# A two-layer hybrid encoder on one core: the phases as a list of smaller steps in another order

## The chip, the cores and the metric

The kernel runs on one core of a Trainium2 chip. The metric is the time of one execution on the device in microseconds, as a median of several runs. A core has five engines that work side by side: TensorE (PE, matrix multiply; its weight loads have a row of their own, PEld), VectorE (DVE), ScalarE (ACT), GpSimd (POOL) and SyncE (SP), whose queue issues nearly all DMA transfers here. Each engine takes its instructions in the order in which the program has them.

## What is computed

Two groups of requests, "prompt" (p, 1024 tokens) and "sample" (s, 512 tokens), go through the same two layers of width 1024. They share the weights and nothing else.

```python
for l in range(DEPTH):                       # 2 layers
    h = rms_norm(x, norm_g[l])
    u = h @ w_in[l]                          # one projection to all branches
    mk, mv = split(rms_norm(mem, ...) @ w_mem_kv[l])
    if l % 2 == 0:
        y1 = short_conv(gb, gc, hc, conv_w)  # gated convolution
        y2 = window_attention(q, k, v, sink) # "swa", 2 kv heads
    else:
        y1 = dense_gqa(q, k, v)              # "ax", 2 kv heads
        y2 = diff_attention(dq, dk, dv, ...) # "diff", 4 heads, two softmaxes each
    ym = memory_attention(mq, mk, mv)        # "mem", 256 memory tokens
    x = x + (concat(y1, y2, ym) * silu(z)) @ w_out[l]
```

## The kernel before

Every fp32 product is made of three matmuls on a high and a low part (whi, wlo of the weights; hi, lo of the activations). A tile that comes by DMA as alo or wraw is split: ScalarE casts it to the high part (line 186), VectorE or GpSimd subtracts (line 187).

The work is written as calls at the end of trunk_kernel. in_proj(g, l, hs, ids, ahead, hfs) makes chunks of 256 columns of the input projection for group g and layer l: kv, q0, q1, z0 to z8, mq, in layer 0 also gch and gbz (the convolution), in layer 1 dk, dq and dv (each 0 and 1). hfs chooses halves of 512 tokens. Each chunk loads four wraw tiles (load_w). q, k, dq, dk and mq go through prep (norm and rotary tables on ScalarE, VectorE and GpSimd), are transposed on TensorE (stT, store_stack), split, and stored to DRAM (st_...); v and dv are stored by put_v, z by silu2.

The attention steps swa, ax, diff and mem_attn load k, v and q from there (k, v, qhh, qll), make scores (s), their maxima (nm, VectorE), exponentials (e, ScalarE), transposes (pT), splits (pthi, ptlo) and outputs (o), and store y. diff(g, hd, half) does head hd, or one half of its query tokens. They are marked urgent. out_proj loads y (load_y, into alo and ahi), multiplies by w_out and adds x. norm_steps makes the normalized and transposed activations for the next layer in twelve small steps per 512 tokens (four loads and scalings, eight groups of four transposes hT, one PSUM buffer, with hg or ht behind); they wait in a list BG. The projections call between() at a quarter of each group of matmuls, which takes one store_stack from TAIL or one step from BG.

ahead is a function that in_proj, out_proj or mem_kv calls ahead of its last chunk: it empties BG and TAIL and loads the next activations. The activation ring "act" has 16 tiles, k and v rings three each, wraw three, the PSUM ring "x" one.

The calls are the program's order as written; a scheduler then makes each engine's order, and takes an urgent step first when it is ready, so that projections fill the room that attention leaves on TensorE.

Of the kernel before, what the change touches and what calls it, by code (L numbers as in the profile page):

```python
# [68 lines left out]
def trunk_kernel(ctx: ExitStack, tc: tile.TileContext, a: dict, dbg=None):  # L69
# [883 lines left out]
    in_proj("p", 0, hp, range(0, 3))  # L953
    swa("p", 0)
    in_proj("p", 0, hp, range(3, 5))
    swa("p", 1)
    in_proj("p", 0, hp, range(5, 7))
    mem_attn("p", 0)
    in_proj("p", 0, hp, range(7, 15), ahead("y0", lambda: load_y("p", 0, 0, slice(0, 4))))
    out_proj("p", 0, 0, nxt["y0"] + load_y("p", 0, 0, slice(4, 5)), ahead("y1", lambda: load_y("p", 0, 1)))  # L960
    BG.extend(norm_steps(rows_of(S["p", "x1"]), put_dram(S["p", 1, "h"], 0, g1)))
    bg(3)
    out_proj("p", 0, 1, nxt["y1"], ahead("m", lambda: load_act(S["m", 1, "h"], range(4))))
    BG.extend(norm_steps(rows_of(S["p", "x1"], 1), put_dram(S["p", 1, "h"], 512, g1)))
    bg(3)
    mem_kv(1, nxt["m"], ahead("hp", lambda: load_h("p", 1)))
    hp = nxt["hp"]
    in_proj("p", 1, hp, range(0, 3))
    ax("p", 0)
    in_proj("p", 1, hp, range(3, 5))  # L970
    ax("p", 1)
# [17 lines left out]
    diff("p", 3, 0)  # L989
    mem_attn("p", 1, 0)  # L990
    out_proj("s", 0, 0, nxt["ys"] + [ym0])
    flush()
    bg(len(BG))
    hs = [new_h()]
    BG.extend(norm_steps(rows_of(S["s", "x1"]), put_act(hs[0], g1)))
    bg(3)
    RATE[0] = 1
# [1 line left out]
    RATE[0] = 1
    diff("p", 2, 1)  # L1000
    diff("p", 3, 1)
    mem_attn("p", 1, 1)
# [9 lines left out]
    diff("s", 3)  # L1012
    ym = [ring(sb, [128, 2, 512], F32R, "xh", f"ym{i}") for i in range(2)]
    mem_attn("s", 1, ys=ym)
    out_proj("p", 1, 0, load_y("p", 1, 0), ahead("y1", lambda: load_y("p", 1, 1)))
    out_proj("p", 1, 1, nxt["y1"], ahead("ys", lambda: load_y("s", 1, 0, slice(0, 4))))
    out_proj("s", 1, 0, nxt["ys"] + [ym])
# [111 lines left out]
```

## Time and profile before

| | us |
|---|---|
| median of 3 runs | 2139.87 (2139.24 to 2140.7) |
| the profiled execution | 2138.74 |
| its span in the trace | 2136.9 |
| TensorE busy in the span | 2055.3 (96%) |
| VectorE busy | 1548.2 (72%) |
| ScalarE busy | 1113.2 (52%) |
| GpSimd busy | 976.6 (46%) |

A busy time is the union of an engine's instructions. The table by stretch gives the same for stretches of the span, with the number of instructions, the granted TensorE clock as a share of full speed, the share of the DMA engines and their rate. The table of waits names the instruction that waited, its line, what ended the wait and its line, the total, the number and the longest. A timeline has the start, the time taken, the engine, the line and the instruction, and in brackets the idle time ahead of it with what ended that.

### The profile page before, as it was taken

To read this page: it belongs to the slowest core of one execution; us is meant where nothing else is said; L and a number is where in the kernel's file an instruction comes from. 1 tells how busy PE (TensorE), PEld (TensorE's weight loads), DVE (VectorE), ACT (ScalarE), POOL (GpSimd) and SP (SyncE) were. 2 spreads that over 40 slices of the span, in tenths; PEclk is the share of its full clock that TensorE was granted. 3 is DMA by queue.
4 is the path that set the end of the run, shared out by engine and by line. 5 is a ranking of instruction groups with operands and counts; after the bars stand their busy time and mean duration, and the time that the engine had idled before them with its cause. 6 is when DMAs were issued, how large, how long until landed. Compare 5 with 4: busy or idle time off the path is not lost. (4 is left out here: it accounts for less than half of the span.)

```text
span 2136.9 us, 40415 instructions
## 1 busy us (share of the span) xinstructions
PE 2055.3 (96%) x14056; PEld 1887.4 (88%) x14056; DVE 1548.2 (72%) x3340; ACT 1113.2 (52%) x2634; POOL 976.6 (46%) x994
## 2 busy tenths in 40 slices
PE   6999999999999999999999999998998999989999
PEld 6999888889999899999998888886997898979999
DVE  8779867654545688976989988777879876866532
ACT  5545433443343466665666655456566565644521
POOL 6753512342124564743745553333345775643311
...
GB/s 232 203 246 198 215 104 89 121 105 221 253 235 211 167 94 100 124 105 131 114 104 204 179 202 161 118 163 226 170 208 172 195 176 191 137 207 242 200 180 105
DMA packets 321052, 363.69 MB, mean 170 GB/s; under 512 B 27984, under 2 KB 227408, under 8 KB 320848
## 3 DMA queue, kind: packets, MB, share of 16 engines
...
q8 instruction: 111, 1.82, 0.4%
...
## 5 line engine op out<-in xcount | busy, mean ns | idle before, releaser
L187 POOL TENSOR_TENSOR wlo<-wraw,whi 128x512 fp32r<-128x512 f32 x182 | 249.1, 1371 | 359.7 <-ACT whi L186 350.4
L682 ACT ACTIVATE e<-s,nm 128x512 f32<-128x512 f32 (+1 forms) x416 | 264.6, 639 | 224.2 <-DVE nm L680 163.5
L186 ACT CAST whi<-wraw 128x512 fp32r<-128x512 f32 x388 | 237.2, 622 | 274.7 <-PE po L311 91.4
L591 DVE TENSOR_TENSOR ptlo<-pT,pthi 128x512 fp32r<-128x512 f32 x352 | 237.6, 682 | 48.8 <-ACT pthi L590 47.5
L680 DVE TENSOR_REDUCE nm<-s 128x1 f32<-128x512 f32 (+1 forms) x368 | 247.7, 681 | 26.5 <-PE s L584 25.3
L309 PE MATMUL po<-whi,ahi 128*128 128x256 f32 x896 | 255.1, 285 | 4.8 <-ACT ahi L186 2.5
L310 PE MATMUL po<-wlo,ahi 128*128 128x256 f32 x896 | 254.3, 285 | 0.0
L311 PE MATMUL po<-whi,alo 128*128 128x256 f32 x896 | 253.5, 285 | 0.6 <-DVE alo L187 0.5
L590 ACT CAST pthi<-pT 128x512 fp32r<-128x512 f32 x352 | 199.8, 587 | 98.1 <-PE pT L670 55.0
L187 DVE TENSOR_TENSOR wlo<-wraw,whi 128x512 fp32r<-128x512 f32 x206 | 165.7, 805 | 105.6 <-ACT whi L186 104.4
L309 PE MATMUL pa<-whi,ahi 128*128 128x256 f32 x768 | 219.7, 286 | 1.8 <-ACT ahi L186 1.1
L310 PE MATMUL pa<-wlo,ahi 128*128 128x256 f32 x768 | 219.3, 286 | 0.3 <-POOL wlo L187 0.3
L311 PE MATMUL pa<-whi,alo 128*128 128x256 f32 x768 | 219.1, 285 | 0.2 <-DVE alo L187 0.2
L223 POOL TENSOR_TENSOR rs<-ss,mhalf 128x8 f32<-128x8 f32 (+2 forms) x108 | 139.7, 1293 | 163.9 <-DVE ss L219 97.2
L583 PE MATMUL s<-k,qhh 128*128 128x512 f32 (+2 forms) x512 | 192.4, 381 | 12.4 <-ACT e L682 10.0
L584 PE MATMUL s<-k,qll 128*128 128x512 f32 (+2 forms) x512 | 183.3, 364 | 4.4 <-DMA qll<-st_s1dq 1.3
L309 PEld LDWEIGHTS po<-whi,ahi 128*128 128x128 f32 x896 | 171.4, 191 | 7.0 <-ACT ahi L186 3.7
L311 PEld LDWEIGHTS po<-whi,alo 128*128 128x128 f32 x896 | 171.1, 192 | 2.2 <-DVE alo L187 1.2
L310 PEld LDWEIGHTS po<-wlo,ahi 128*128 128x128 f32 x896 | 171.4, 192 | 1.0
L323 PE MATMUL pb<-h,whi 128*128 128x512 f32 x432 | 171.2, 396 | 0.0
L325 PE MATMUL pb<-h,wlo 128*128 128x512 f32 x432 | 170.4, 395 | 0.0
L324 PE MATMUL pb<-h,whi 128*128 128x512 f32 x432 | 170.3, 394 | 0.0
...
## 6 DMA issues: line engine op xcount, KB each, us to landing
...
alo<-y_p SPq DMA_DIRECT2D x20, 512.0 KB, 4.8
...
k<-st_p1dk SPq DMA_DIRECT2D x14, 512.0 KB, 4.8
v<-dv_p SPq DMA_DIRECT2D x14, 512.0 KB, 5.7
...
```

Source lines behind the costliest of these rows:

```text
L186: nc.scalar.copy(out=out_hi, in_=src)
L187: lo_eng.tensor_tensor(out=out_lo, in0=src, in1=f32(out_hi), op=ALU.subtract)
L309: nc.tensor.matmul(out=out, lhsT=h, rhs=wh, start=(k == 0), stop=False)
L310: nc.tensor.matmul(out=out, lhsT=h, rhs=wl, start=False, stop=False)
L311: nc.tensor.matmul(out=out, lhsT=l_, rhs=wh, start=False, stop=(k == n - 1))
L323: nc.tensor.matmul(out=out, lhsT=wh, rhs=h, start=(k == 0), stop=False)
L583: nc.tensor.matmul(out=out, lhsT=q2[0], rhs=k, start=True, stop=False)
L584: nc.tensor.matmul(out=out, lhsT=q2[1], rhs=k, start=False, stop=True)
L590: nc.scalar.copy(out=hi, in_=ps)
L591: nc.vector.tensor_tensor(out=lo, in0=ps, in1=f32(hi), op=ALU.subtract)
L680: nc.vector.tensor_reduce(out=nm, in_=s, axis=AXL.X, op=ALU.max, negate=True)
L682: nc.scalar.activation(out=e[:, j, :], in_=s[:, j, :], func=ACTF.Exp, bias=nm[:, j:j + 1], accum_out=su[:, j:j + 1],)
```

## The change

The calls become a list of strings, STEPS, that a function step reads in turn. What was a whole call is cut smaller and put in another order; the functions that do the work are the same.

- diff p 0 runs as two halves, the second first, with its own loads of k and v for each half.
- In the prompt group's layer 1, dv0 comes ahead of ax p 1, dq0 and z4 behind it, dq1 and dv1 behind the halves of diff, dk1 behind z6 of half 0.
- In the sample group's layer 0, diff p 1 1 moves from between q1 and swa s 1 to behind mem s 0; the load of the prompt group's second half (load p 1 1) ahead of gbz3.
- In the sample group's layer 1, dv0 comes first, ahead of mem p 1 1; dk0 stands beside q1 and z2; dk1, dq1, mq0, dv1, z8 and z6 follow diff s 1 in this order.
- The loads that ahead made ahead of the last chunk are steps of their own (load, loady), mostly a chunk earlier. What ahead did ahead of z8 of the prompt group's half 1 (empty BG) is gone, so that the norm's steps for the sample group spread over mq0, z8 and dv0.

```diff
+STEPS = [
+    "in p 0 kv0+q0+z4", "swa p 0", "in p 0 q1+z6+mq0", "swa p 1", "in p 0 z8", "mem p 0",
+    "in p 0 gch0+gbz0+gch1+gbz1+gch2+gbz2", "loady p 0 0 0 4", "in p 0 gch3+gbz3", "loady p 0 0 4 5",
+    "loady p 0 1", "out p 0 0", "norm p 0", "out p 0 1", "norm p 1", "load m", "load p 1 01", "memkv m",
+    "in p 1 kv0+q0+z0", "ax p 0", "in p 1 q1+z2+dk0+dv0", "ax p 1", "in p 1 dq0+z4", "diff p 0 1", "diff p 0 0",
+    "diff p 1 0", "in p 1 dq1+dv1", "in p 1 z6 0", "in p 1 dk1", "in p 1 mq0+z8 0", "load s 0 0",
+    "in s 0 kv0+q0+z4", "swa s 0", "in s 0 q1+z6", "swa s 1", "in s 0 mq0+z8", "mem s 0", "diff p 1 1",
+    "in s 0 gch0+gbz0+gch1+gbz1+gch2+gbz2+gch3", "load p 1 1", "in s 0 gbz3", "loady s 0 0 0 4", "in p 1 z6 1",
+    "diff p 2 0", "diff p 3 0", "mem p 1 0", "out s 0 0", "norm s", "in p 1 mq0+z8 1", "diff p 2 1", "diff p 3 1",
+    "in s 1 dv0", "mem p 1 1", "in s 1 kv0+q0+z0", "ax s 0", "in s 1 q1+dk0+z2+dq0", "ax s 1", "in s 1 z4",
+    "diff s 0", "diff s 1", "loady p 1 0", "in s 1 dk1+dq1+mq0+dv1+z8+z6", "diff s 2", "diff s 3", "mem s 1",
+    "loady p 1 1", "out p 1 0", "loady s 1 0 0 4", "out p 1 1", "out s 1 0",
+]
...
-    in_proj("p", 1, hp, range(5, 9))
-    diff("p", 0)
-    diff("p", 1, 0)
-    in_proj("p", 1, hp, range(9, 12))
-    in_proj("p", 1, hp, range(12, 15), ahead("hs", lambda: load_h("s", 0)), hfs=[0])
-    hs = nxt["hs"]
-    in_proj("s", 0, hs, range(0, 3))
-    swa("s", 0)
-    in_proj("s", 0, hs, range(3, 5))
-    diff("p", 1, 1)
-    swa("s", 1)
-    in_proj("s", 0, hs, range(5, 7))
...
-    mem_attn("s", 0, ys=ym0)
-    in_proj("s", 0, hs, range(7, 15), ahead("h1", lambda: load_half("p", 1, 1)))
-    in_proj("p", 1, [None, nxt["h1"]], range(12, 13), ahead("ys", lambda: load_y("s", 0, 0, slice(0, 4))), hfs=[1])
-    diff("p", 2, 0)
...
-    in_proj("p", 1, [None, nxt["h1"]], range(13, 15), ahead("", lambda: None), hfs=[1])
...
-    in_proj("s", 1, hs, range(0, 3))
-    ax("s", 0)
-    in_proj("s", 1, hs, range(3, 5))
-    ax("s", 1)
-    in_proj("s", 1, hs, range(5, 9))
-    diff("s", 0)
-    diff("s", 1)
-    in_proj("s", 1, hs, range(9, 15))
-    diff("s", 2)
...
+    def settle():
+
+        bg(len(BG))
+        flush()
...
+        elif op == "loady":
+            settle()
+            l, hf = int(x[0]), int(x[1])
+            part = slice(int(x[2]), int(x[3])) if len(x) > 2 else slice(0, 5)
+            YS.setdefault((g, l, hf), []).extend(load_y(g, l, hf, part))
```

What that does to the engines' orders is seen at three places. Each row is one instruction, or some equal ones that follow each other: its line, what it does, out<-in and the size.

The first is SP's queue around out s 0 0, where alo<-y_s are the loads of the attention outputs of the sample group's layer 0 (y_s_119), st_p1dq and dv_p belong to diff p 2 0, and y_s_119<-yo stores the last outputs. Before:

```order
L106 DMA y_s_119<-yo 128x2x128
L106 DMA zg_p_106<-z_19135 128x512
L106 DMA wraw<-in_w_out_dram 128x512 x2
L106 DMA alo<-y_s_119 128x1024
L106 DMA wraw<-in_w_out_dram 128x512
L106 DMA qhh<-st_p1dq_96 64x2x256
L106 DMA k<-st_p1dk_98 128x1024
L106 DMA qhh<-st_p1dq_96 64x2x256
L106 DMA qll<-st_p1dq_96 64x2x256 x2
L106 DMA alo<-y_s_119 128x1024
```

After:

```order
L119 DMA wraw<-in_w_out_dram 128x512 x2
L119 DMA alo<-y_s_119 128x1024
L119 DMA qhh<-st_p1dq_96 64x2x256 x2
L119 DMA qll<-st_p1dq_96 64x2x256 x2
L119 DMA alo<-y_s_119 128x1024
L119 DMA wraw<-in_w_out_dram 128x512 x3
L119 DMA alo<-y_s_119 128x1024
L119 DMA y_s_119<-yc 128x512
L119 DMA wraw<-in_w_out_dram 128x512
L119 DMA alo<-y_s_119 128x1024
```

The attention's stores (yo) stood between the loads before; now the last of them are further up, and the loads stand close to each other, with only the convolution's store (yc) ahead of the last.

The second is TensorE's order where the norm of the sample group's second layer (hT) meets the second half of diff p 2 (s, pT) and mem p 1 (o). Before:

```order
L253 MATMUL hT<-ident_r,x 128x128 x4
L583 MATMUL s<-k,qhh 128x512
L584 MATMUL s<-k,qll 128x512
L887 MATMUL o<-pthi,v 128x512
L887 MATMUL o<-ptlo,v 128x512
L887 MATMUL o<-pthi,v 128x512
L799 MATMUL pT<-ident_r,e 128x128 x7
L887 MATMUL o<-ptlo,v 128x512
L583 MATMUL s<-k,qhh 128x512
L584 MATMUL s<-k,qll 128x512
L253 MATMUL hT<-ident_r,x 128x128 x4
```

After (h_20858 and its like are tiles of the activations that this norm makes, pa is in s 1 dv0):

```order
L266 MATMUL hT<-ident_r,x 128x128 x4
L322 MATMUL pa<-whi,h_20858 128x256
L323 MATMUL pa<-wlo,h_20858 128x256
L900 MATMUL o<-pthi,v 128x512
L900 MATMUL o<-ptlo,v 128x512
L900 MATMUL o<-pthi,v 128x512
L900 MATMUL o<-ptlo,v 128x512
L898 MATMUL pT<-ident_r,e 128x128 x4
L812 MATMUL pT<-ident_r,e 128x128
L324 MATMUL pa<-whi,h_20859 128x256
L322 MATMUL pa<-whi,h_20858 128x256
L323 MATMUL pa<-wlo,h_20858 128x256
```

The groups of transposes stand further apart, and matmuls of dv0 that read what they make now stand between them.

The third is SP's queue where the sample group's dq1 is stored (st_s1dq_123<-sthi, stlo) and the weights of the chunks behind it are loaded (wraw<-in_w_in). Before:

```order
L106 DMA st_s1dq_123<-sthi 128x1x256 x2
L106 DMA st_s1dq_123<-stlo 128x1x256 x2
L106 DMA zg_s_133<-z_25191 128x512
L106 DMA qhh<-st_s1dq_123 64x2x256 x2
L106 DMA qll<-st_s1dq_123 64x2x256 x2
L106 DMA st_s1dq_123<-sthi 128x1x256 x2
L106 DMA st_s1dq_123<-stlo 128x1x256 x2
L106 DMA qhh<-st_s1dq_123 64x2x256
L106 DMA y_s_134<-yo 128x256
L106 DMA qhh<-st_s1dq_123 64x2x256
L106 DMA qll<-st_s1dq_123 64x2x256 x2
L106 DMA zg_s_133<-z_25246 128x512
```

After (st_s1dq_122 is dq0, stored long ahead):

```order
L119 DMA wraw<-in_w_in_dram 128x512 x3
L119 DMA y_s_134<-yo 128x2x128
L119 DMA wraw<-in_w_in_dram 128x512
L119 DMA st_s1dq_123<-sthi 128x1x256 x2
L119 DMA st_s1dq_123<-stlo 128x1x256 x2
L119 DMA qhh<-st_s1dq_122 64x2x256 x2
L119 DMA qll<-st_s1dq_122 64x2x256 x2
L119 DMA zg<-zg_s_133 128x2x128
L119 DMA y_s_134<-yo 128x2x128
L119 DMA wraw<-in_w_in_dram 128x512
```

The loads of dq1 stood right behind its stores before, with the weights behind them; now the loads behind the stores are those of another tensor, and weights stand on both sides.

## Rows read from the trace of the kernel before

**Rows 1.** The page: span, and each engine's busy time, share and instructions.

```profile
span 2136.9 us, 40415 instructions
...
PE 2055.3 (96%) x14056; PEld 1887.4 (88%) x14056; DVE 1548.2 (72%) x3340; ACT 1113.2 (52%) x2634; POOL 976.6 (46%) x994
```

**Rows 2.** By stretch: length, busy PE, PEld, DVE, ACT, POOL, clock, DMA share, GB/s.

```profile
0.00:660.00 660.00, 629.98 (x4073) 572.71 (x4074) 444.12 (x921) 292.44 (x674) 253.61 (x253) 0.99 0.61 186
660.00:1130.00 470.00, 466.75 (x3408) 440.04 (x3407) 370.47 (x858) 282.96 (x668) 260.69 (x284) 1.00 0.45 128
1130.00:1230.00 100.00, 96.24 (x643) 86.72 (x642) 91.58 (x208) 66.17 (x162) 54.85 (x49) 1.00 0.60 179
1230.00:1440.00 210.00, 204.05 (x1137) 173.43 (x1136) 172.35 (x411) 107.42 (x270) 87.62 (x80) 1.00 0.57 162
1450.00:1490.00 40.00, 31.71 (x180) 24.66 (x179) 30.87 (x76) 24.49 (x61) 10.52 (x14) 1.00 0.73 218
1597.00:1627.00 30.00, 22.03 (x96) 15.59 (x94) 29.84 (x53) 20.89 (x50) 16.76 (x14) 0.84 0.71 209
1660.00:1710.00 50.00, 47.19 (x333) 43.32 (x332) 40.20 (x84) 29.03 (x79) 39.88 (x43) 1.00 0.68 188
1803.00:1815.00 12.00, 9.45 (x69) 8.74 (x68) 4.90 (x12) 4.52 (x11) 3.48 (x5) 1.00 0.92 263
1880.00:1905.00 25.00, 19.12 (x128) 17.83 (x127) 10.10 (x22) 8.44 (x19) 4.13 (x6) 0.93 0.74 213
...
1130.00:2040.00 910.00, 865.61 (x5805) 781.88 (x5804) 707.49 (x1528) 518.63 (x1262) 448.06 (x446) 0.99 0.63 184
```

**Rows 3.** Waits of TensorE, 1440 to 1500: waiter, releaser, total, times, longest.

```profile
PE po L309 <- ACT ahi L186: 2.5, 2, 1.4
PE o L887 <- DVE yo L891: 2.4, 1, 2.4
```

**Rows 4.** Timeline of TensorE in the last out_proj: start, time taken, instruction.

```profile
2091.86 0.28 PE L309 MATMUL po<-whi,ahi 128*128 128x256 f32 x1
2091.98 0.28 PE L310 MATMUL po<-wlo,ahi 128*128 128x256 f32 x1
```

**Rows 5.** Waits of TensorE, 1590 to 1700.

```profile
PE hT L253 <- DVE hg L264: 3.5, 2, 3.1
```

**Rows 6.** Timeline of VectorE beside the norm, from 1611.

```profile
1611.45 0.68 DVE L264 TENSOR_TENSOR hg<-hT,gains 128x512 f32<-128x512 f32 x1
...
1616.31 0.41 DVE L279 TENSOR_TENSOR h<-hg,h 128x256 fp32r<-128x256 f32 x1
```

**Rows 7.** Timeline of SP's queue, 1886 to 1896.

```profile
1886.83 1.25 SPq L106 DMA_DIRECT2D st_s1dq<-sthi  x2
...
1894.13 1.45 SPq L106 DMA_DIRECT2D wraw<-in_w_in_dram  x3
```

**Rows 8.** Waits of TensorE, 1790 to 2030.

```profile
PE ss L816 <- ACT zg L810: 4.5, 1, 4.5
...
PE s L584 <- DMA qll<-st_s1dq: 1.3, 1, 1.3
```

**Rows 9.** Timeline of ScalarE, two casts of weights that waited.

```profile
1812.00 0.62 ACT L186 CAST whi<-wraw 128x512 fp32r<-128x512 f32 x1 [7.13 <-DMA wraw<-in_w_in_dram]
...
1899.81 0.62 ACT L186 CAST whi<-wraw 128x512 fp32r<-128x512 f32 x1 [7.62 <-DMA wraw<-in_w_in_dram]
```

**Rows 10.** DMA issues: count, KB each, median us to landing.

```profile
k<-st_p1dk SPq DMA_DIRECT2D x14, 512.0 KB, 4.8
...
alo<-y_s SPq DMA_DIRECT2D x8, 512.0 KB, 6.3
```

**Rows 11.** VectorE's groups, 1110 to 1290: count, busy us, mean ns.

```profile
L680 DVE TENSOR_REDUCE nm<-s 128x1 f32<-128x512 f32 x42 | 28.4, 679 | 0.2 <-PE s L584 0.2
L789 DVE SCALAR_TENSOR_TENSOR e<-e,sx 128x512 f32<-128x512 f32 x22 | 20.2, 927 | 2.5 <-POOL e L786 2.5
L591 DVE TENSOR_TENSOR ptlo<-pT,pthi 128x512 fp32r<-128x512 f32 x29 | 19.6, 678 | 2.5 <-ACT pthi L590 2.5
```

More of the change, by code (lines that the diff above doesn't have):

```diff
@@ L952, in trunk_kernel @@
     BG.extend([lambda n=n: rope_table(n) for n in TABS[2:]])
[L953 to L971, printed above, removed]
-    in_proj("p", 1, hp, range(5, 9))
-    diff("p", 0)
-    diff("p", 1, 0)
-    in_proj("p", 1, hp, range(9, 12))
@@ L976, in trunk_kernel @@
-    in_proj("p", 1, hp, range(12, 15), ahead("hs", lambda: load_h("s", 0)), hfs=[0])
-    hs = nxt["hs"]
-    in_proj("s", 0, hs, range(0, 3))
-    swa("s", 0)
-    in_proj("s", 0, hs, range(3, 5))
-    diff("p", 1, 1)
-    swa("s", 1)
-    in_proj("s", 0, hs, range(5, 7))
-    ym0 = [ring(sb, [128, 2, 512], F32R, "xh", f"ym{i}") for i in range(2)]
-    mem_attn("s", 0, ys=ym0)
-    in_proj("s", 0, hs, range(7, 15), ahead("h1", lambda: load_half("p", 1, 1)))
-    in_proj("p", 1, [None, nxt["h1"]], range(12, 13), ahead("ys", lambda: load_y("s", 0, 0, slice(0, 4))), hfs=[1])
@@ L988, in trunk_kernel @@
-    diff("p", 2, 0)
[L989 to L997, printed above, removed]
-    in_proj("p", 1, [None, nxt["h1"]], range(13, 15), ahead("", lambda: None), hfs=[1])
[L999 to L1002, printed above, removed]
-    in_proj("s", 1, hs, range(0, 3))
-    ax("s", 0)
-    in_proj("s", 1, hs, range(3, 5))
@@ L1006, in trunk_kernel @@
-    ax("s", 1)
-    in_proj("s", 1, hs, range(5, 9))
-    diff("s", 0)
-    diff("s", 1)
-    in_proj("s", 1, hs, range(9, 15))
-    diff("s", 2)
[L1012 to L1017, printed above, removed]
+    H = {("p", 0): hp}
@@ new lines, in trunk_kernel, with step @@
+    YS, YM = {}, {}
+    def settle():
+        bg(len(BG))
+        flush()
+    def step(op, g, *x):
+        if op == "in":
+            l = int(x[0])
+            ids = [CHUNKS[l].index((c.rstrip("0123456789"), int(c.lstrip("abcdefghijklmnopqrstuvwxyz")))) for c in x[1].split("+")]
+            in_proj(g, l, H[g, l], ids, hfs=[int(h) for h in x[2]] if len(x) > 2 else None)
+        elif op == "swa":
+            swa(g, int(x[0]))
+        elif op == "ax":
+            ax(g, int(x[0]))
+        elif op == "diff":
+            diff(g, int(x[0]), int(x[1]) if len(x) > 1 else None)
+        elif op == "mem":
+            l = int(x[0])
+            if g == "s":
+                YM[l] = [ring(sb, [128, 2, 512], F32R, "xh", f"ym{i}") for i in range(2)]
+                mem_attn("s", l, ys=YM[l])
+            else:
+                mem_attn(g, l, int(x[1]) if len(x) > 1 else None)
+        elif op == "norm":
+            if g == "s":
+                H["s", 1] = [new_h()]
+                settle()
+                BG.extend(norm_steps(rows_of(S["s", "x1"]), put_act(H["s", 1][0], g1)))
+            else:
+                hf = int(x[0])
+                BG.extend(norm_steps(rows_of(S["p", "x1"], hf), put_dram(S["p", 1, "h"], 512 * hf, g1)))
+            bg(3)
+        elif op == "load":
+            settle()
+            if g == "m":
+                H["m"] = load_act(S["m", 1, "h"], range(4))
+            else:
+                l, hfs = int(x[0]), [int(h) for h in x[1]]
+                H.setdefault((g, l), [None] * (GROUPS[g] // 512))
+                H[g, l] = [load_half(g, l, hf) if hf in hfs else None for hf in range(GROUPS[g] // 512)]
+        elif op == "loady":
+            settle()
+            l, hf = int(x[0]), int(x[1])
+            part = slice(int(x[2]), int(x[3])) if len(x) > 2 else slice(0, 5)
+            YS.setdefault((g, l, hf), []).extend(load_y(g, l, hf, part))
+        elif op == "memkv":
+            mem_kv(1, H["m"])
+        elif op == "out":
+            l, hf = int(x[0]), int(x[1])
+            out_proj(g, l, hf, YS[g, l, hf] + ([YM[l]] if g == "s" else []))
+        elif op == "settle":
+            settle()
@@ L1018, in trunk_kernel @@
+    for s in STEPS:
+        step(*s.split())
     in_order(tc, chains)
```

## The prediction

> **What bounds the kernel now.** I read four views in turn. The page's engine table comes first: TensorE is busy for 2055.3 of 2136.9 us, VectorE for 1548.2 [rows 1]. The kernel is bound by TensorE, and a new order can win only where TensorE waits. The second view is the table by stretch [rows 2]. From 660 to 1130 TensorE is 466.75 of 470.00 us busy: there nothing is to be had. Idle time sits in a few stretches: 3.76 us in 1130:1230, 5.95 in 1230:1440, 8.29 in 1450:1490, 7.97 in 1597:1627 (where the granted clock was also down to 0.84), 2.81 in 1660:1710, 2.55 in 1803:1815 and 5.88 in 1880:1905. The third view, the waits of TensorE in such a stretch, names who was late [rows 3, 5, 8]. The fourth, the timeline of the engine that was late, says why [rows 6, 7, 9].
>
> The pace of TensorE at work is read from two neighbouring matmuls of 128x256: they start 0.12 us apart [rows 4], though one is shown as 0.28 long. I count one such matmul as 0.12 us, one of 128x512 as twice that (an estimate), and one of a group of 128x128 transposes as 0.1.
>
> The weight loads give another measure of headroom. The row PEld stands at 1887.4 us, 88% of the span [rows 1]. The Trainium skill (Perfetto Trace Analysis, Identifying the Most-Contended Engine) wants TensorE judged by the busy share of LDWEIGHTS and not of matmuls; by it 249.5 us would be idle and the kernel could fall towards 1890 us. Here that overstates the room: from 660 to 1130 PEld is 440.04 of 470 us busy [rows 2] while TensorE loses only 3.25: ten times as much idle time in the row of the loads as in that of the matmuls. It changes no term below.
>
> **What the change does, part by part.** The engines do the same instructions; only four DMAs are added. Up to the first projections of layer 1 of the prompt group, some 660 us, the order of every engine is the same but for a few rows. The idle 30 us in 0:660 [rows 2] therefore stay. 660:1130 has no idle time to lose. What counts lies between 1130 and 2040, where TensorE is busy for 865.61 of 910 us and so idle for 44.4 [rows 2].
>
> *Term 1, the attention outputs of the sample group.* In before, swa s 1 and mem s 0 run late, beside diff p 2 0, and the loads alo<-y_s for out s 0 0 stand in SP's queue behind the y_s stores of swa s 1. Counted in the order of the whole program, the second to fourth of them stand 19, 28 and 24 matmuls ahead of their first use, 3 to 4.5 us, while such a load lands 6.3 us after its issue [rows 10] and is then split by ScalarE and VectorE. TensorE waits for ahi for 2.5 us and for yo of mem s 0 for 2.4 [rows 3]; with the smaller waits it is idle for 8.29 us of the stretch [rows 2]. The change runs diff p 1 1 behind mem s 0 instead of ahead of swa s 1, so all outputs are stored earlier; the four loads stand 64, 51, 47 and 54 matmuls ahead (many of 128x512), 8 to 14 us. I take **-8**; bounds -2.5 (the ahi wait alone) and -8.3.
>
> *Term 2, the norm of the sample group's second layer.* In 1597:1627 VectorE is 29.84 of 30 us busy, and TensorE waits 3.5 us for hg [rows 2, 5]; it is idle for 7.97. Eight groups of four hT transposes share one PSUM buffer, and each must wait for hg of the one before. In before the last five groups span 87 matmuls (15 us) with 57 VectorE instructions, 29.7 us at the means of their groups: 14.6 too many. In the change the same five span 135 matmuls (18.4 us) with 48 VectorE instructions (25.0 us): 6.6 too many. That is 8.0 us less. But the change lets the norm's last steps run inside in s 1 dv0, whose matmuls read the h tiles at once: five links, whose first reader stands 17 to 44 matmuls behind the transposes, 2 to 5 us. In before the way from the start of hg at 1611.45 to the end of its h subtraction (1616.31 + 0.41) took 5.3 us [rows 6]. With half a microsecond lost per link, 2.5 us come back. I take **-5.5**; bounds -8, and +8 (all five links short by 3.2 us, with nothing else gained).
>
> *Term 3, weights queued behind stores and loads.* SP issues in order. From 1886 to 1894 its row is st_s1dq stores, qhh and qll loads that must wait for those stores, stores again, loads again; the next wraw goes out at 1894.13 [rows 7]. ScalarE's next cast in line, of whi, then waits 7.62 us, and sq and yo of diff s 0 (line 810) stand behind it [rows 9]; TensorE waits 4.5 us for them and 1.3 for qll [rows 8]. The same picture ends at 1812.00, with 7.13 us of waiting in ScalarE [rows 9]; TensorE loses 2.55 us around it, in ax s 1 [rows 2]. The change puts dk1 and dq1 ahead of mq0, dv1, z8 and z6, and dk0 ahead of ax s 1, so that a head's stores are long done when its loads come; weights no longer stand behind them. In SP's order of before 20 loads of q, k and v of the sample group's layer 1 follow a store to the same tensor within nine rows and 4 us of matmuls; in that of the change one does. I take **-8** (4.5 + 1.3 + 2.55, rounded down); bounds 0 and -11 (with the 2.81 us of 1660:1710, the same chain for q0).
>
> *Term 4, the first heads of diff beside dk1.* diff p 0 is cut in halves, and dk1, mq0 and z8 of half 0, and the first projections of the sample group now run beside it. From the first score of diff p 0 to the last of diff p 1 half 0, before has 1153 matmuls (163.2 us) and 367 VectorE instructions (161.6 us at group means such as 679 ns for nm, 678 for ptlo and 927 for e [rows 11]). The change has 1245 (172.6 us) and 403 (179.0 us): 92 matmuls or 9.4 us more, VectorE 17.4 us more. VectorE goes from level with TensorE to 6.4 us above it. I take the difference, **+8**. The bounds: 0, if it is covered as in 660:1130 (VectorE 370.47 of 470 busy and hardly a wait), and the upper end below.
>
> The upper end: e<-e,sx, with both inputs in SBUF, takes 927 ns where ptlo of the same 128x512, with one input in PSUM, takes 678 [rows 11], and GpSimd's work in this stretch grows from 79 instructions to 100. If each of these 21 lengthens one VectorE instruction by the 0.25 us between those rows, 5 us come on top: **+13**. The Trainium skill (GPSIMD Engine Reference, Key points) says that GpSimd shares its SBUF interfaces with VectorE and contends with instructions that have two SBUF inputs. The difference between the two rows agrees with it; by that rule alone term 4 would be +13 and not +8, which is a part of the first rival.
>
> *Term 5, four DMAs more.* The halves of diff p 0 load k and v twice: two tiles of each, 512 KB a tile, 4.8 us to landing for one of k [rows 10]. k and v have three buffers, a head needs two of each, so the second k and v of the second half wait for the first half's end, as at every change of head in before, where the price is inside idle times such as the 3.76 us of 1130:1230. I take **+0.5**; bounds 0 and +4.
>
> **Sum.** -8 - 5.5 - 8 + 8 + 0.5 = -13. Against the profiled execution's own 2138.74 us (span 2136.9) that is 2125.7. The median of the runs, 2139.87, lies 1.1 us higher, so I say **2127 us**, 0.6% faster. What a measurement of this kernel tells from no change is about 0.2%, 4.3 us.
>
> **The rivals.**
> *VectorE becomes the bound (slower).* In the stretch of term 4 VectorE has 179.0 us of work for 172.6 us of TensorE, and in dv0 the norm stands directly in TensorE's path. If both go to their ends, +13 and +8, the sum with terms 1, 3 and 5 as above is -8 - 8 + 13 + 8 + 0.5 = +5.5: **2145**. With terms 1 and 3 at half it would be 2153. It decides against the change once the two VectorE places together cost more than the 16 us that terms 1 and 3 give back. For it: 91.58 of 100 us busy in 1130:1230 with TensorE already losing 3.76 [rows 2]. Against it: the peaks of VectorE at 1450 and 1600 get lower by the same moves.
> *The waits only move (no change).* Attention on ScalarE and VectorE is in order; what TensorE no longer waits for in 1450:1490 and 1880:1905 it waits for in the next chain of scores, whose waits (for e, the exponentials) are not touched. Then terms 1 and 3 come to half, -8, against +8: **2140**.
> *All of it comes (faster still).* Term 4 is covered and the norm costs nothing new: -8 - 8 - 8 = -24, some more in 1230:1440: **2114**.
> *The change does not do what it says:* ruled out, the order differs as described.
>
> **Chances.** The forecast, 2118 to 2134: 0.48. Faster still: 0.16. Waits only move: 0.14. VectorE bound: 0.22. So faster by over 0.2% 0.64, within it 0.13, slower 0.23. The range reaches down to all the lower bounds together and half of the idle time in 1230:1440 (-8 - 8 - 11 - 3 = -30: 2110), and up to the slower rival and half of what lies between its two cases, 2149; outside it I leave some 0.15.
>
> **What would show it.** Term 1: no wait of po for ahi at the start of out s 0 0, four alo<-y_s loads on SP before the stretch of diff p 2 0. Term 2: hT's wait for hg under 2 us in all, and pa of dv0 waiting for h or h's split, under 4 us. Term 3: ScalarE's waits for wraw<-in_w_in_dram, 7.62 us at the longest, under 4 us after 1780; no wait of ss for ACT zg. Term 4: VectorE over 95% busy for some 100 us after 1110, with TensorE idle 8 us more there than before. I am wrong if that stretch loses over 20 us, if pa of dv0 waits over 8 us, or if new waits for wraw stand where dk1 to z6 follow in one row.

## The result, and the profile after

| | before | changed |
|---|---|---|
| median, us | 2139.55 | 2106.52 |
| lowest to highest, us | 2134.26 to 2140.7 | 2099.39 to 2114.58 |
| ratio | 1 | 0.9854, interval 0.9831 to 0.9877 |

The kernel became 33 us faster; I had forecast 13, and 2106.5 lies below the range of 2110 to 2149. The direction was right, the size was not. The profiled execution of the changed kernel, 2099.39 us, is the fastest of its four.

The head of its page answers to [rows 1]:

```profile
span 2097.6 us, 40483 instructions
...
PE 2040.2 (97%) x14056; PEld 1885.0 (90%) x14056; DVE 1552.4 (74%) x3340; ACT 1115.9 (53%) x2634; POOL 969.9 (46%) x994
```

The span is 39.3 us shorter. Only 24.2 us of that are idle time (81.6 before, 57.4 after): the other 15 are busy time of TensorE with the same 14056 matmuls. A matmul of 128x256 is shown as 0.28 us long, and the next can start 0.12 us after it [rows 4], so that a wait of up to 0.16 us between two starts doesn't show as idle time; and in 1597:1627 the granted clock was down to 0.84 [rows 2]. Idle time alone, on which my sum was built, is therefore too small a measure of the loss. I also count, for each matmul, the time to the start of the next one less the pace of its shape (0.12 us for 128x256, 0.23 for 128x512, about 0.1 for a 128x128 transpose, read from neighbouring matmuls), and sum that up. By this count 142 us were lost before and 103 after. As the matmuls are the same, these totals differ by what the spans differ; what the count adds is in which stretch the time is lost.

The table by stretch, first for the changed kernel. The columns are those of [rows 2]; the last three rows below it are of the kernel before in the same stretches:

```profile
545.00:660.00 115.00, 109.36 (x902) 107.38 (x900) 62.39 (x100) 47.89 (x87) 32.90 (x29) 1.00 0.81 266
660.00:1130.00 470.00, 467.47 (x3383) 439.18 (x3384) 370.49 (x861) 283.19 (x670) 250.54 (x277) 1.00 0.44 125
1130.00:1230.00 100.00, 93.91 (x642) 85.53 (x641) 95.80 (x208) 65.31 (x157) 65.78 (x61) 1.00 0.67 204
1440.00:1550.00 110.00, 108.99 (x856) 105.19 (x856) 90.37 (x226) 65.87 (x174) 44.77 (x49) 1.00 0.63 193
1550.00:1650.00 100.00, 93.75 (x645) 85.64 (x644) 88.38 (x197) 67.06 (x169) 54.36 (x57) 0.97 0.65 189
1750.00:1900.00 150.00, 148.10 (x1047) 137.71 (x1045) 114.28 (x215) 88.08 (x193) 85.31 (x83) 1.00 0.70 202
```

```profile
1440.00:1550.00 110.00, 101.71 (x709) 91.27 (x709) 86.95 (x208) 66.00 (x171) 41.69 (x48) 1.00 0.66 197
1550.00:1650.00 100.00, 91.09 (x612) 80.97 (x611) 83.95 (x180) 65.89 (x166) 51.29 (x55) 0.95 0.65 190
...
1750.00:1900.00 150.00, 141.76 (x1026) 132.45 (x1024) 105.57 (x207) 84.26 (x190) 85.47 (x85) 1.00 0.59 172
```

From 1440 to 1550, where the loads for out s 0 0 were late, TensorE now starts 856 matmuls where it started 709. From 1130 to 1230 it is idle for 6.1 us instead of 3.8 [rows 2], VectorE being busy for 95.80 of 100. From 1750 to 2010 these are the three longest waits that are left (two more are of 0.4 and 0.3 us), against 4.5 us for zg in one wait before [rows 8]:

```profile
PE s L596 <- ACT e L695: 1.9, 1, 1.9
PE rbT L847 <- DVE yo L838: 0.8, 1, 0.8
PE ss L829 <- ACT zg L823: 0.8, 1, 0.8
```

### The profile page after: what moved, and what is told of

Its sections match the earlier page's. It is cut to its first block, busy times and chain, and to the rows that moved or that the text cites. A ratio compares the mean times of both kernels' runs of the same rounds, so it can differ in the third digit from the quotient of the medians.

```text
span 2097.6 us, 40483 instructions
## 1 busy us (share of the span) xinstructions
PE 2040.2 (97%) x14056; PEld 1885.0 (90%) x14056; DVE 1552.4 (74%) x3340; ACT 1115.9 (53%) x2634; POOL 969.9 (46%) x994
## 4 chain that ended last, share of the span: by engine, by line
PE 75%; DMA 7%; DVE 7%; issue 3%; POOL 2%; ACT 1%; SPq 1%; DVEq 0%; POOLq 0%; ACTq 0%
PE pb L338 8%; PE pb L336 8%; PE pb L337 8%; PE pa L323 5%; PE pa L324 5%; PE pa L322 5%; PE po L322 4%; PE po L323 4%; PE po L324 4%; PE s L596 4%; PE s L597 4%; PE o L754 3%; PE pT L750 3%; PE o L685 1%; PE pT L683 1%
## 5 line engine op out<-in xcount | busy, mean ns | idle before, releaser
L200 DVE TENSOR_TENSOR wlo<-wraw,whi 128x512 fp32r<-128x512 f32 x206 | 170.8, 830 | 95.3 <-ACT whi L199 92.5
```

The source lines that it names most:

```text
L200: lo_eng.tensor_tensor(out=out_lo, in0=src, in1=f32(out_hi), op=ALU.subtract)
```

## The experiments

Two ways of cutting the change apart were used: to undo one part in the changed kernel, and to make one part alone in the kernel before. Each was timed against the kernel before on the same chip. There were three chips, with medians of the kernel before from 2135.9 to 2139.2, so rows of different chips are compared by their ratios.

| | kernel | median, us | ratio to before | interval |
|---|---|---|---|---|
| e0 | changed, again | 2107.5 | 0.9863 | 0.9841 to 0.9884 |
| e1 | changed, diff p 1 1 back (term 1) | 2125.2 | 0.9945 | 0.9923 to 0.9966 |
| e2 | changed, norm and dv0 back (term 2) | 2109.5 | 0.9872 | 0.9851 to 0.9893 |
| e3 | changed, s layer 1 back (term 3) | 2110.1 | 0.9881 | 0.9860 to 0.9901 |
| e4 | changed, p layer 1 back (terms 4, 5) | 2111.9 | 0.9882 | 0.9860 to 0.9904 |
| e6 | changed, early loads back | 2113.9 | 0.9894 | 0.9872 to 0.9915 |
| e5 | before, diff p 1 1 moved | 2101.4 | 0.9834 | 0.9814 to 0.9855 |
| e11 | the same again | 2101.0 | 0.9823 | 0.9802 to 0.9844 |
| e14 | before, diff p 1 1 one step later still | 2100.9 | 0.9832 | 0.9808 to 0.9857 |
| e12 | e5 and term 2 | 2106.5 | 0.9857 | 0.9832 to 0.9881 |
| e13 | e5 and term 3 | 2106.3 | 0.9860 | 0.9834 to 0.9885 |
| e9 | e5 and terms 2 and 3 | 2106.9 | 0.9855 | 0.9835 to 0.9875 |
| e10 | e5, z6 of half 1 later | 2108.4 | 0.9860 | 0.9838 to 0.9881 |
| e7 | before, mq0 of half 1 earlier | 2130.6 | 0.9972 | 0.9959 to 0.9984 |
| e8 | before, diff p 1 1 half the way | 2146.4 | 1.0039 | 1.0021 to 1.0057 |

And the loss of TensorE against its pace, by my count, in us, each from one profiled execution. The stretches are in each kernel's own time, so that one stretch doesn't hold quite the same work in each:

| stretch | before | changed | e0 | e5 | e1 | e8 |
|---|---|---|---|---|---|---|
| 0 to 545 | 30.6 | 29.7 | 33.9 | 32.0 | 32.4 | 29.2 |
| 545 to 675 | 16.1 | 9.3 | 14.2 | 10.1 | 14.6 | 14.4 |
| 675 to 1250 | 23.6 | 26.1 | 24.3 | 25.4 | 24.6 | 24.3 |
| 1250 to 1440 | 9.0 | 4.3 | 5.4 | 7.8 | 5.6 | 5.4 |
| 1440 to 1550 | 14.4 | 3.1 | 1.3 | 2.0 | 12.6 | 23.4 |
| 1550 to 1750 | 24.9 | 20.4 | 18.9 | 19.8 | 20.3 | 22.7 |
| 1750 to the end | 23.6 | 10.1 | 10.2 | 9.4 | 18.5 | 26.7 |

**The changed kernel again, and each part undone.** First the kernel itself:

> The changed kernel unaltered, for a time beside the variants on the same chip and a second profile. The trace of the first profile shows 103 us in which TensorE runs below its pace, against 142 before, at a profiled time of 2099.39; the four runs went from 2099 to 2115. If the spread comes from the clock, a run at a mean clock of 0.992 should be 8 to 12 us longer than one at 0.997 with the same waits: about 2107. If it comes from waits that fall differently, the clock of the profiles will be equal and other stretches will show the idle time.

It came out at 2107.5. The count of its loss is some 5 us higher than in the first profile, with 9.1 us more up to 675 and some 4 less behind: the first profile was a lucky one in the part that the change hardly touches. The first four executions of the changed kernel went from 2099 at a clock of 0.997 to 2115 at 0.992, but another was at 2108 with the lowest clock, 0.991: the clock alone doesn't order them, and whether it causes waits or follows them isn't told apart.

Term 1 undone:

```diff
-    "in s 0 q1+z6", "swa s 1", "in s 0 mq0+z8", "mem s 0", "diff p 1 1",
+    "in s 0 q1+z6", "diff p 1 1", "swa s 1", "in s 0 mq0+z8", "mem s 0",
```

> The changed kernel with diff p 1 1 put back ahead of swa s 1 (the step of term 1 undone, all else as changed). If term 1 is worth what its own stretch shows (13.3 us lost in 1450:1500 before, 1.0 at the same work after), this kernel is 12 us slower than the changed one, about 2118, and its trace shows waits for ahi and yo ahead of and in out s 0 0 again. As I had put it in the prediction it is 8 us slower, 2114. If waits only move, because swa s 1 with a late diff p 1 1 is kept waiting somewhere else anyway, it is within 4 us of the changed kernel.

It cost 17.7 us, more than any of the three said. Waits are back in the stretch, of those that I had named the one for ahi, at half its size, and not the one for yo. These are the three longest (columns of [rows 3]):

```profile
1440.00:1550.00 110.00, 103.58 (x730) 94.07 (x730) 89.52 (x210) 67.11 (x175) 39.85 (x50) 0.98 0.67 203
```

```profile
PE s L596 <- ACT e L695: 2.0, 3, 1.2
PE po L322 <- ACT ahi L199: 1.2, 1, 1.2
PE s L597 <- DMA qll<-st_p1mq: 1.1, 1, 1.1
```

By the count 11.3 us are lost there against e0, and another 8.3 from 1750 on, with the changed order of chunks in place. So the one move acts in two places. And without it the rest of the change isn't worthless: e1 is still 11.2 us faster than the kernel before on its chip (2136.4), where I had summed up 5 for that rest. In its one profile it loses 4.6 us less than the kernel before from 1550 to 1750, and 5.1 less from 1750 on.

Term 2 undone:

```diff
-    "diff p 2 0", "diff p 3 0", "mem p 1 0", "out s 0 0", "norm s", "in p 1 mq0+z8 1", "diff p 2 1", "diff p 3 1",
-    "in s 1 dv0", "mem p 1 1", "in s 1 kv0+q0+z0", "ax s 0", "in s 1 q1+dk0+z2+dq0", "ax s 1", "in s 1 z4",
+    "diff p 2 0", "diff p 3 0", "mem p 1 0", "out s 0 0", "norm s", "in p 1 mq0 1", "settle s", "in p 1 z8 1", "diff p 2 1", "diff p 3 1",
+    "mem p 1 1", "in s 1 kv0+q0+z0", "ax s 0", "in s 1 q1+dk0+z2+dq0", "ax s 1", "in s 1 dv0+z4",
```

> The changed kernel with the norm of the sample group's second layer emptied ahead of z8 of half 1 again, and dv0 of the sample group back behind ax s 1 (the step of term 2 undone). By the prediction 5.5 us slower, about 2112. By the two traces the losses around the norm are 20.6 us before and 18.9 after, so that it is only 2 us slower. If the first reader of the norm in dv0 costs more than the spreading gives, it is faster, by up to 5 us (2101).

2.0 us slower, inside the intervals, as the second answer has it. Its profiled execution (2112.2, above its median) does lose more beside the norm than e0: some 9 us from 1550 to 1750 by the count. The rows for 1550 to 1650, first e0, then e2:

```profile
1550.00:1650.00 100.00, 92.92 (x654) 85.19 (x653) 88.07 (x194) 67.68 (x174) 55.31 (x60) 0.98 0.69 208
1550.00:1650.00 100.00, 90.21 (x601) 81.13 (x600) 87.09 (x196) 67.11 (x171) 58.43 (x63) 0.95 0.63 189
```

Term 3 undone:

```diff
-    "in s 1 dv0", "mem p 1 1", "in s 1 kv0+q0+z0", "ax s 0", "in s 1 q1+dk0+z2+dq0", "ax s 1", "in s 1 z4",
-    "diff s 0", "diff s 1", "loady p 1 0", "in s 1 dk1+dq1+mq0+dv1+z8+z6", "diff s 2", "diff s 3", "mem s 1",
+    "in s 1 dv0", "mem p 1 1", "in s 1 kv0+q0+z0", "ax s 0", "in s 1 q1+z2", "ax s 1", "in s 1 dk0+dq0+z4",
+    "diff s 0", "diff s 1", "loady p 1 0", "in s 1 dk1+dq1+dv1+z6+mq0+z8", "diff s 2", "diff s 3", "mem s 1",
```

> The changed kernel with the sample group's layer 1 in the old order of chunks (dk0, dq0, z4 behind ax s 1; dk1, dq1, dv1, z6, mq0, z8 behind diff s 1; dv0 stays early): the step of term 3 undone. By the prediction 8 us slower, about 2114. By the two traces TensorE loses 25 us from the second half of mem p 1 to the last out_proj before and 12 us after: 12 us slower, 2118, and the waits for zg and for qll stand in the trace again. If the queue of SP isn't the cause but the early end of the attention ahead of it, it is within 3 us of the changed kernel.

2.5 us slower, inside the intervals: the third answer, and nothing like the 8 or 12 us. Here too the profiled execution (2114.1, above its median) loses more in the stretch of its term than e0, some 7 us from 1750 on. The rows for 1750 to 2030, first e0, then e3:

```profile
1750.00:2030.00 280.00, 276.38 (x2078) 263.90 (x2077) 195.35 (x359) 150.30 (x336) 132.36 (x135) 0.99 0.66 198
1750.00:2030.00 280.00, 273.41 (x2027) 259.29 (x2026) 194.82 (x358) 148.61 (x333) 133.84 (x136) 0.99 0.65 198
```

Terms 4 and 5 undone, and the early loads:

```diff
-    "in p 1 kv0+q0+z0", "ax p 0", "in p 1 q1+z2+dk0+dv0", "ax p 1", "in p 1 dq0+z4", "diff p 0 1", "diff p 0 0",
-    "diff p 1 0", "in p 1 dq1+dv1", "in p 1 z6 0", "in p 1 dk1", "in p 1 mq0+z8 0", "load s 0 0",
+    "in p 1 kv0+q0+z0", "ax p 0", "in p 1 q1+z2", "ax p 1", "in p 1 dk0+dq0+dv0+z4", "diff p 0",
+    "diff p 1 0", "in p 1 dk1+dq1+dv1", "in p 1 z6+mq0+z8 0", "load s 0 0",
```

> The changed kernel with the prompt group's layer 1 in the old order of chunks and diff p 0 whole (the steps of terms 4 and 5 undone). By the prediction, where these cost 8 and 0.5 us, it is 8 us faster than the changed kernel, about 2099. By the traces, where TensorE loses 13.4 us from 1100 to 1250 before and 15.4 after, it is 2 us faster. If the new order beside diff p 0 itself gains, because chunks run earlier and leave less to do beside the sample group, it is slower.

```diff
-    "in p 0 gch0+gbz0+gch1+gbz1+gch2+gbz2", "loady p 0 0 0 4", "in p 0 gch3+gbz3", "loady p 0 0 4 5",
-    "loady p 0 1", "out p 0 0", "norm p 0", "out p 0 1", "norm p 1", "load m", "load p 1 01", "memkv m",
+    "in p 0 gch0+gbz0+gch1+gbz1+gch2+gbz2+gch3", "loady p 0 0 0 4", "in p 0 gbz3", "loady p 0 0 4 5",
+    "out p 0 0 loady:p:0:1", "norm p 0", "out p 0 1 load:m", "norm p 1", "memkv m load:p:1:01",
...
```

> The changed kernel with the loads of layer 0's outputs and of the activations up to 660 us back ahead of the last chunk of the call before. I had counted this at nothing. The first profile of the changed kernel lost 39.0 us up to 660 us and the one of before 46.6, the second of the changed kernel 43.9 at 650. If it is chance and the clock, this kernel is within 2 us of the changed one. If the earlier rows in SP's queue count, 4 to 7 us slower.

Both are slower than e0, by 4.4 and 6.3 us, though I had term 4 as a cost; they ran on another chip, and their intervals overlap that of e0. But e6 loses nothing where its loads are (13.8 us from 545 to 675 by the count, against 14.2 in e0); it loses 7.7 us more than e0 from 1100 to 1440, far behind them. An early edit lets the scheduler come to another order of the instructions behind it, and that seems to be worth a few us either way. Undone one at a time, the parts other than term 1 give 2 to 6 us. For e2 and e3 one profile each puts a loss where the term stands, for e6 it lies elsewhere; as two profiles of one kernel differ by 9.1 us up to 675 alone, that settles none of them.

**One part alone.** The same move as in e1, made by itself in the kernel before:

```diff
     in_proj("s", 0, hs, range(3, 5))
-    diff("p", 1, 1)
     swa("s", 1)
...
     mem_attn("s", 0, ys=ym0)
+    diff("p", 1, 1)
```

> The kernel before with nothing changed but diff p 1 1, which goes from ahead of swa s 1 to behind mem s 0. Undone in the changed kernel this step cost 17.7 us by the medians. If it stands alone, the kernel before gains 15 to 18 us, about 2120. If it needs the other steps (the waits that it removes are taken up by the old order of the sample group's layer 1 and by the norm), it gains 8 us at most, as I had put the term itself.

It gave 36 us, all of the gain and a little more, and twice what the higher of the two answers said; the repetition (e11) was to show that this isn't chance, and gave the same:

> The kernel before with only diff p 1 1 moved, once more, beside the three others. If the first result (2101.4, 36 us faster) is not chance: 2099 to 2104.

Its stretches, and all its waits of TensorE over 0.2 us from 1430 to 1550 (one) and over 0.6 from 1750 to 2050 (two):

```profile
545.00:660.00 115.00, 110.27 (x909) 108.16 (x908) 61.46 (x98) 47.25 (x85) 30.26 (x26) 1.00 0.79 259
...
1440.00:1550.00 110.00, 109.69 (x849) 105.33 (x848) 93.24 (x231) 67.06 (x172) 42.40 (x44) 1.00 0.62 189
1550.00:1650.00 100.00, 92.06 (x608) 82.28 (x607) 90.62 (x190) 66.81 (x169) 65.97 (x67) 0.97 0.64 191
...
1750.00:1900.00 150.00, 149.37 (x1057) 138.96 (x1057) 113.75 (x217) 88.83 (x197) 82.35 (x81) 1.00 0.68 204
```

```profile
PE o L806 <- DVE ptlo L591: 0.3, 1, 0.3
...
PE o L805 <- ACT pthi L590: 1.4, 1, 1.4
PE pT L885 <- DVE ptlo L591: 1.2, 1, 1.2
```

The waits for zg and qll from which I had built term 3 [rows 8] are gone, although the sample group's layer 1 still runs in its old order. Why is read from where the two kinds of work stand. The first rows are of the kernel before: the first matmul of out s 0 0, the first score of diff p 2 1, the first matmul of in s 1 kv0 and the first of out p 1 0. Then the same four in e5:

```profile
1456.30 0.36 PE L309 MATMUL po<-whi,ahi 128*128 128x256 f32 x1
...
1563.37 0.40 PE L583 MATMUL s<-k,qhh 128*128 128x512 f32 x1
...
1630.85 0.28 PE L309 MATMUL pa<-whi,h 128*128 128x256 f32 x1
...
1923.82 0.28 PE L309 MATMUL po<-whi,ahi 128*128 128x256 f32 x1
```

```profile
1443.81 0.28 PE L309 MATMUL po<-whi,ahi 128*128 128x256 f32 x1
...
1562.20 0.40 PE L583 MATMUL s<-k,qhh 128*128 128x512 f32 x1
...
1594.96 0.39 PE L309 MATMUL pa<-whi,h 128*128 128x256 f32 x1 [2.08 <-DVE z L435]
...
1886.20 0.28 PE L309 MATMUL po<-whi,ahi 128*128 128x256 f32 x1
```

The attention stands at the same time in both (1563.4 and 1562.2). The projections start out s 0 0 12.5 us earlier and, as that runs almost without waits and the norm behind it ends sooner, the next layer's first chunk 35.9 us earlier and the last group of out_proj 37.6 us earlier. The lead that they win is kept to the end. It also pays a second time: with projections ahead, a head's q, k and v are stored long ahead of the attention that loads them. Counted in the order of the program, loads of q, k and v in the sample group's layer 1 that follow a store to the same tensor within 4 us were 20 before; they are 8 in e5 with the old order of chunks, and 39 in e1 with the new order. What makes many close pairs is the missing lead, more than the order of chunks.

**What the move must pass.** The move could act through swa s 1, from which diff p 1 1 takes VectorE, or through mem s 0, the last step that out s 0 0 needs:

```diff
-    diff("p", 1, 1)
     swa("s", 1)
+    diff("p", 1, 1)
```

> The kernel before with diff p 1 1 between swa s 1 and mem s 0, halfway to its new place. Theory of the lead: out s 0 0 cannot start at full pace until mem s 0 is stored, and all projections stand behind it; so what counts is that diff p 1 1 (some 80 us of attention) is behind the last step that out s 0 0 needs. Halfway, mem s 0 ends as late as before (1476 against 1421 with the whole move), and the kernel gains 4 us at most: 2134 or more. Rival: swa s 1 and diff p 1 1 disturb each other on VectorE, and it is their order that counts; then most of the 36 us come with half the move: 2119 or less.

```profile
1440.00:1550.00 110.00, 99.97 (x679) 88.67 (x677) 89.63 (x217) 66.21 (x185) 42.96 (x59) 0.94 0.62 183
...
1750.00:1900.00 150.00, 140.45 (x1015) 132.21 (x1014) 106.59 (x201) 83.26 (x181) 90.38 (x87) 0.98 0.58 168
```

At 2146.4 it is slower than before. swa s 1 runs as early as in e5 (its last matmul at 1389), but mem s 0 ends at 1481, as late as before (1476), and out s 0 0 lasts until 1577. So it is mem s 0 that counts, and the rival, the order of swa s 1 and diff p 1 1, is out. One step later than in the change, nothing more is won:

```diff
     diff("p", 2, 0)
+    diff("p", 1, 1)
     diff("p", 3, 0)
```

> The kernel before with diff p 1 1 one step later still, behind diff p 2 0. Theory of the lead: once diff p 1 1 is behind mem s 0, nothing of the projections waits for it until out p 1 0 and 1, so its place among the prompt group's heads is of no account: 2098 to 2105. If each step later gains: 2095 or less; if the heads' k and v (diff p 1 1 reads other tensors than diff p 2 0) cost at the changes: 2107 or more.

2100.9, as the lead has it. More cover without the move:

```diff
     mem_attn("p", 1, 0)
+    in_proj("p", 1, [None, nxt["h1"]], range(13, 14), hfs=[1])
     out_proj("s", 0, 0, nxt["ys"] + [ym0])
```

> The kernel before with mq0 of the prompt group's half 1 (96 matmuls of 128x256, 11.5 us) ahead of out s 0 0 instead of behind it, and diff p 1 1 left in its old place. If what counts at 1450:1490 is that TensorE has nothing to do until the late attention of the sample group is through, the 11.5 us of cover take 8 to 11 us off there, and the kernel gains most of that. If the attention that is late stays late behind out s 0 0, and the cover is missing beside the norm, it gains less than 4 us.

It gained 7.0 us, between the two answers. Below are its rows for 1440 to 1550 and 1590 to 1640, then its two largest waits from 1590 to 1640, then the kernel before in the second stretch:

```profile
1440.00:1550.00 110.00, 106.19 (x764) 98.20 (x763) 89.14 (x200) 67.97 (x170) 47.91 (x48) 1.00 0.66 195
1590.00:1640.00 50.00, 33.92 (x157) 27.28 (x156) 42.98 (x91) 30.85 (x76) 18.82 (x21) 0.80 0.47 156
```

```profile
PE s L583 <- ACT e L682: 9.3, 5, 3.4
PE pa L309 <- DVE z L435: 4.4, 1, 4.4
```

```profile
1590.00:1640.00 50.00, 42.03 (x227) 33.93 (x226) 49.60 (x103) 34.61 (x85) 27.49 (x25) 0.90 0.63 188
```

The cover does its work at 1440 (3.8 us idle instead of 8.3) and is missing beside the norm, where 16 us are idle and the granted clock is 0.80: part of the time, behind waits of up to 3.4 us, it stood at the lower of the two levels, 1.2 GHz. Cover that is shifted pays in one place and takes in another; attention that is shifted behind what the projections need does not.

**The other terms on top of the move.**

```diff
-    in_proj("p", 1, [None, nxt["h1"]], range(13, 15), ahead("", lambda: None), hfs=[1])
+    in_proj("p", 1, [None, nxt["h1"]], range(13, 15), hfs=[1])
...
+    in_proj("s", 1, hs, [7])
     mem_attn("p", 1, 1)
...
-    in_proj("s", 1, hs, range(5, 9))
+    in_proj("s", 1, hs, [5, 6, 8])
```

> The kernel before with diff p 1 1 moved and the step of term 2 (dv0 early, the norm spread). With terms 2 and 3 together the kernel was at 2106.9, 6 us above diff p 1 1 alone. If it is the norm in dv0's path that costs it, as I had feared for term 2: about 2106. If term 2 is worth its 5.5 us: 2096. If it neither costs nor gains: 2099 to 2103.

```diff
-    in_proj("s", 1, hs, range(3, 5))
+    in_proj("s", 1, hs, [3, 5, 4, 6])
...
-    in_proj("s", 1, hs, range(5, 9))
-    in_proj("s", 1, hs, range(9, 15))
+    in_proj("s", 1, hs, [7, 8])
+    in_proj("s", 1, hs, [9, 10, 13, 11, 14, 12])
```

> The kernel before with diff p 1 1 moved and the step of term 3 (the sample group's chunks in the new order, dv0 as before). If the weights behind stores still cost their 8 us with diff p 1 1 moved: 2093. If the waits are gone with the projections' lead: 2099 to 2103. If the new order costs the 6 us that terms 2 and 3 cost together: about 2107.

Each adds about 5 us to e5. With both in one kernel (e9) it is 5.5:

> The kernel before with diff p 1 1 moved and the steps of terms 2 and 3 as well (dv0 early and the norm spread, the sample group's chunks in the new order), but the prompt group's layer 1 and its loads as before. If the terms add up as I had put them, 13.5 us below the 2101 of diff p 1 1 alone: 2088. If what they remove is gone already with diff p 1 1 moved, the same as it alone within 4 us: 2097 to 2105.

e12 and e13 came out where their answers had a cost, e9 just above both of its own. The intervals of the three overlap those of e5, e11 and e14 in part. That neither term gains on top of the move is shown. That they cost some 5 us is likely and not settled, and where the time would go isn't found: the profiled executions of e12 and e13 (spans of 2102.6 and 2102.0 us) are only 1 to 3.5 us longer than those of e5, e11 and e14 (2101.1, 2100.2 and 2099.1), and from 1550 to 1650, beside the norm that was to cost it, TensorE is idle for 7.44 us in e12 and for 7.94 in e5.

Last, an attempt at more, with the cover beside the norm where e5 still loses 15.2 us:

```diff
-    in_proj("p", 1, [None, nxt["h1"]], range(12, 13), ahead("ys", lambda: load_y("s", 0, 0, slice(0, 4))), hfs=[1])
+    ahead("ys", lambda: load_y("s", 0, 0, slice(0, 4)))()
...
-    in_proj("p", 1, [None, nxt["h1"]], range(13, 15), ahead("", lambda: None), hfs=[1])
+    in_proj("p", 1, [None, nxt["h1"]], range(12, 15), ahead("", lambda: None), hfs=[1])
```

> The kernel before with diff p 1 1 moved, and z6 of the prompt group's half 1 behind out s 0 0 instead of ahead of it (48 matmuls of 128x512, 11.5 us). With diff p 1 1 moved TensorE loses 15 us from 1550 to 1650, beside the norm; z6 is cover there that out s 0 0 no longer needs. If cover is what lacks, up to 8 us faster than diff p 1 1 alone: 2093. Against it: the loads of the outputs for out s 0 0 lose their own cover, 3 to 6 us, and then it is 2098 to 2104.

By the count 1550 to 1650 falls to 8.4 us as hoped, but 1250 to 1440 and 1440 to 1550 rise from 7.8 and 2.0 to 11.3 and 4.7; at 2108.4 nothing is won, and both answers were too low. The best version is the kernel before with the one call moved, at 2101: faster than the changed kernel by some 5 us, by ratios that were taken against the kernel before on different chips. On one chip e14 is 6.6 us below e0 (2100.9 and 2107.5).

## Why the prediction was wrong

Two steps failed above all: the bound of term 1, and the sum, which took the terms as independent.

**Term 1** had the right mechanism and a wrong size: -8 in the sum, -36 alone (e5), -17.7 with the other parts in place (e1). I had bounded it by the idle time of its own stretch, 8.29 us [rows 2]. Two things were left out. From 1440 to 1550 the loss against pace fell by 12.4 us (14.4 to 2.0), as busy rows hide a part of it. And the projections' lead runs on: from 1750 to the end another 14.2 us went (23.6 to 9.4), and some 5 from 1550 to 1750. For these I had written other terms. My bound was no bound: a wait that holds up everything behind it in one kind of work has no upper end in its own stretch.

**The sum.** I added terms 1, 2 and 3 up as if each had a loss of its own. The move alone takes off 36 us and the rest without the move 11.2 (e1 against the kernel before), but both together only 29 (e0; 33 in the first measurement): the rest acts on losses that the move removes too. Terms 4 and 5 and the early loads come to nothing between them: e9, which lacks them, is at 2106.9 (ratio 0.9855) and e0, which has them, at 2107.5 (0.9863).

**Term 2** shows in its own stretch and doesn't arrive at the end. I had -5.5; on top of the move it is about +5 (e12), undone it is 2.0 (e2). The losses beside the norm, in 1550 to 1650, are 17.6 us before, 12.8 and 12.6 in the two profiles of the changed kernel, 15.2 in e5. The signs that I had named did come: waits of hT for hg are below the 0.2 us that the view shows, and pa waits 0.7 for h. But other waits grew. Here are TensorE's for the exponentials and for ptlo from 1550 to 1650, first before, then in the changed kernel:

```profile
PE s L583 <- ACT e L682: 2.7, 3, 1.4
PE pT L799 <- DVE ptlo L591: 1.2, 2, 0.8
```

```profile
PE s L596 <- ACT e L695: 3.4, 4, 2.3
PE pT L898 <- DVE ptlo L604: 1.9, 1, 1.9
```

So of the 3.5 us for hg [rows 5] 1.4 came back there, and 2.8 in e0: the second rival (the waits only move), here in one place. VectorE is busy for 88.38 of 100 us there and was for 83.95 before; that it is the reason was not tried.

**Term 3** took a symptom for a cause. The rows were read rightly: the weights did stand behind stores and loads in SP's queue [rows 7, 9]. But those stores and loads stood close since the attention had caught up with its own projections; e5 removes the waits without touching the order. Nor are the close pairs the price: e1 has twice as many as the kernel before and loses 5.1 us less from 1750 on, and e3, with the move, loses some 7 us more there than e0 and has no wait for qll over 0.2 us. What the new order gives without the move isn't explained by them. My sign, no wait of ScalarE for wraw over 4 us after 1780, was met, in e5 too (rows of ScalarE's waits from 1750 to 2030, before and e5):

```profile
ACT whi L186 <- DMA wraw<-in_w_in_dram: 17.1, 4, 7.6
```

```profile
ACT whi L186 <- DMA wraw<-in_w_in_dram: 9.1, 3, 3.9
```

A sign that two theories share proves neither. The other sign, no wait of ss for zg, the changed kernel missed by 0.8 us, and e5 met it.

**Term 4** was +8 and is about nothing, by e9 and e0 above and by the count: from 675 to 1440 it has 32.6 us before, 30.4 and 29.7 in the changed kernel. e4, with it undone, is 4 us slower. The stretch did get heavier for VectorE, as counted. Here are 1110 to 1290 in the changed kernel and before:

```profile
1110.00:1290.00 180.00, 171.43 (x1192) 158.02 (x1192) 168.14 (x380) 110.08 (x266) 106.09 (x97) 0.99 0.63 187
```

```profile
1110.00:1290.00 180.00, 171.78 (x1152) 154.77 (x1152) 159.08 (x372) 108.13 (x267) 89.47 (x81) 1.00 0.64 188
```

VectorE has 9.1 us more, GpSimd 16.6, and TensorE gets through 40 matmuls more in the same time. My sign came by half: VectorE is over 95% busy from 1130 to 1230, but TensorE's idle time from 1110 to 1290 goes from 8.22 to 8.57 us and not up by 8. The step that failed is the subtraction: it took VectorE's work less TensorE's for a loss, and no such loss came. VectorE was busy for 93% there, so it still had time left; that this is why is argued, not tried. Its bound of 0 was the right value. The upper end was too high as well: of the three groups of [rows 11], the one with two inputs in SBUF, e, takes 987 ns instead of 927, the other two are unchanged:

```profile
L693 DVE TENSOR_REDUCE nm<-s 128x1 f32<-128x512 f32 x40 | 27.1, 678 | 0.0
L802 DVE SCALAR_TENSOR_TENSOR e<-e,sx 128x512 f32<-128x512 f32 x22 | 21.6, 987 | 0.8 <-POOL e L799 0.6
L604 DVE TENSOR_TENSOR ptlo<-pT,pthi 128x512 fp32r<-128x512 f32 x26 | 17.5, 681 | 0.4 <-ACT pthi L603 0.3
```

That is 22 times 60 ns, 1.3 us, where I had 5. The Trainium skill (GPSIMD Engine Reference, Key points) has GpSimd contend with VectorE's instructions that have two SBUF inputs; the row agrees in kind. In the other profiles e takes 953 ns in e0, and 929 and 867 in e5 and e4 with the old order. Another group with two inputs in SBUF, alo<-alo,ahi, goes from 696 to 812 ns (16 of them, 1.9 us), but it takes 816 in e4 too, so that this rise doesn't come with the order of the stretch. Whether GpSimd is the cause of either was not tried.

**Term 5**, four DMAs more, can't be told from nothing. **The first 660 us** I had left at no change, and that holds in time, if not in every row: the kernel before shows 545 to 660 at 106.81 us busy, e5 with the same order of that part at 110.27, so that 3.5 us lie between two executions of the same work. By the count 7.7 of the 39 us between the first two profiles lie ahead of 675; in e0, with 48.1 us lost there against 46.7 before, nothing of it is left.

**The rivals.** VectorE as the bound (2145), which I had given 0.22, did not come, nor did no change (2140), though waits did move beside the norm. "All of it comes" (2114, 0.16) was the nearest in number, and for a wrong reason: it let three terms add up, where one alone brings all.
